# A fused two-part transformer kernel: modulation loads issued singly, four mixer products ahead of the norm, a fixed order in the router, and one more projection of layer 1 from the un-normed x

## The chip, the cores and the metric

One core of one Trainium2 chip runs the whole program. The metric is the device time of one execution in microseconds; the kernel before was timed three times. All products are made on TensorE (PE), elementwise work on VectorE (DVE) and ScalarE (ACT), a few copies on GpSimd (POOL). SyncE (SP) issues the weight loads, POOL's queue the modulation loads.

## The reference, cut to what matters

The input x is 256 tokens by 1024. It passes two hybrid layers, a final norm, one mixer block and one mixture of experts (MoE). All of it is float32.

```python
# one hybrid layer (twice)
mod = silu(c) @ ada_w + ada_b                       # six vectors: sh_m, sc_m, g_m, sh_f, sc_f, g_f
h = rms_norm(x, norm_mix_g) * (1 + sc_m) + sh_m
proj = h @ w_in                                     # NA, MLA and GQA inputs, three gates
o_na, o_mla, o_gqa = ...                            # three kinds of attention
merged = sigmoid(ga)*(o_na @ w_br_na) + sigmoid(gb)*(o_mla @ w_br_mla) + sigmoid(gc)*(o_gqa @ w_br_gqa)
x = x + g_m * (merged @ w_out)
h = rms_norm(x, norm_ffn_g) * (1 + sc_f) + sh_f
gate, up = split(h @ ffn_w_gate_up)
x = x + g_f * ((silu(gate) * up) @ ffn_w_down)
# after both layers
x = rms_norm(x, final_norm_g)
# mixer: RG-LRU, gated delta rule (GDN), stick-breaking attention, gated linear attention (GLA)
m = sum_n sigmoid(merge_n) * (y_n @ w_branch[n]);  x = layer_norm(alpha*x + m @ w_out)
# MoE: 16 experts in 4 groups; the best group, then the top 2 experts in it
scores = sigmoid(x @ w_router);  y = sum over chosen e of w_e * (silu(x@w_gate[e]) * (x@w_up[e])) @ w_down[e]
out = layer_norm(alpha*x + y)
```

In the mixer, the GDN input passes a causal convolution of four taps before its chunked recurrence, and so does the RG-LRU input.

## The kernel before, in words

**Products.** Activations lie transposed, 1024 features as eight slices of 128 partitions by 256 tokens. A float32 product is made of three matmuls: each operand is split into a high part rounded to the PE's format and a low part, the rest (`mm3`). A block of 128 output columns is 8 slices by 3 matmuls of 256 tokens, so 24; a load of 256 columns is 48. Products go to PSUM tiles of one bank; the tags are mm (two buffers), s (two), t (two), o and ad (one each).

**Weights.** `raw` has SP load up to 1 MB into one of three slots (`wr`); `pieces` makes the high part on ACT (a cast, into one of five `wh` slots) and the low part on DVE (a subtraction, into one of five `wl` slots). A raw slot is free for the next load when the subtraction has read it. `load` does both for 256 columns. Three lists change the order: `s.behind` holds a piece's cast behind a given instruction, `s.hold` holds the next subtractions behind given instructions, `s.defer` collects subtractions that are issued later.

**Order.** A list scheduler puts each engine's instructions into one order when the program is built; at run time an engine takes them in that order and waits for data and for slots. `s.after` adds an order without a wait. `post` and `step` put generators (attention, heads) between the blocks of a projection.

**Modulation.** The vectors of layer 0 that are needed first come from matmuls; the others from `ada`: a load of 0.5 MB on POOL's queue into one of ten `big` slots, and one DVE multiply and sum. `tick`, called by every `raw`, advances the generator; here two loads (`pace` 2) in each tick, in the order of the program on POOL, where the four copies of kg stand as well.

**Layer 1's start.** `norm_add` has already prepared z = x times gain, in high and low parts, with two extra columns for the shift. `zblock` multiplies a weight with z and afterwards scales the result by r = 1/rms; the shift's product comes out of column 256 and is added on ACT by the caller. So these products need no norm. `rstd` makes r from a matmul by Ln and Exp on ACT and a Newton step of three DVE operations (L252 to L254). In layer 1 the MLA latents are made that way; the GQA, NA and gate projections use the normed h from `norm_parts`.

**Layer 1's attention.** The GQA projection has three blocks, then NA's q and k (evacuated at L734) and v. `s.behind = evac` holds the casts of w_uq and w_ukv behind the evacuation of NA's k; the weights of the gates and of the next projection (labelled L_att in the profile) follow.

**Mixer.** `final_norm` writes z times r over x in eight slices, each with its splits; r lives in a `wl` slot. The two RG blocks multiply the un-normed z and scale by r (L1492). The misc block (beta, decay and low-rank columns) does so too, but in bank mm, after them; GDN's six blocks use the normed x.

**Router.** `out_norm` makes both token blocks' layer norm, the router's logits and the start of the MoE sum (matmuls with alpha times the identity). `route` chooses experts on DVE with some twenty small operations; `moe` builds placement matrices P and gathers tokens by matmul. Subtractions of the first experts' weights were deferred and are issued among them.

## Time and profile before

| | us |
|---|---|
| median of three runs | 1578.55 (1578.36 to 1579.76) |
| profiled execution | 1578.81 |
| its span, first to last instruction | 1577.1 |
| PE busy in the span | 1515.9 (96%) |
| DVE busy | 1199.1 (76%) |
| ACT busy | 902.7 (57%) |

The mean granted clock of PE was 0.986 of full speed. Busy times are of one execution; L12 is line 12 of the kernel. In a timeline, a row has the start, the time taken by all of the x instructions in the row, engine, line, operation, output and inputs, and in brackets how long the engine had been idle and what ended that. PEclk is the clock granted to PE, 1.00 being full speed.

### The profile page before, as it was taken

The page shows a single profiled execution, that of the slowest core. Times are in us where ns is not written, and L with a number is a line of the kernel's source. Part 1 is how long each engine was busy: PE and PEld are TensorE (multiplying, and loading weights), DVE is VectorE, ACT ScalarE, POOL GpSimd, SP SyncE. Part 2 cuts the span into 40 slices and gives each one's busy share as a digit, 9 for nine tenths or more (in the row PEclk, how much of TensorE's full clock was granted, in tenths as well). Part 3 has the DMA queues.
Part 4 walks back from the last instruction along what each step waited for, and adds up shares of the span by engine and source line. Part 5 has one row for each costly group of instructions (what it writes and reads, how often), then busy time and mean ns, then how long its engine had stood idle before and what let it go on. Part 6 is the DMA issues. An engine that isn't in the chain of part 4 may idle for free.

```text
span 1577.1 us, 27664 instructions
## 1 busy us (share of the span) xinstructions
PE 1515.9 (96%) x11216; PEld 1397.5 (89%) x11216; DVE 1199.1 (76%) x1760; ACT 902.7 (57%) x1316; POOL 100.7 (6%) x173
## 2 busy tenths in 40 slices
PE   6999999999997999999998999999999899999996
PEld 5889999999986989999997989989999688888884
DVE  5899789776785997975558875566666798888896
ACT  5565555444563554644446662675555477777774
POOL 0211000000001110000000022122000000000000
PEclk9999999999998999999999999999999999999998
DMA  9879676876446876565554640335656499999992
GB/s 348 283 238 305 198 240 200 308 267 215 134 141 231 288 241 212 183 208 188 187 174 143 188 126 9 117 103 157 186 175 227 160 324 330 330 330 331 332 346 79
DMA packets 206197, 346.27 MB, mean 220 GB/s; under 512 B 6944, under 2 KB 175024, under 8 KB 193776
## 3 DMA queue, kind: packets, MB, share of 16 engines
q1 hardware_dynamic: 191040, 294.42, 56.0%
q0 software_dynamic: 12656, 46.16, 8.3%
q10 hardware_dynamic: 2368, 3.86, 0.7%
q8 instruction: 90, 1.47, 0.4%
q14 instruction: 43, 0.35, 0.1%
HBM read 343.36 MB, written 1.05 MB: 218 GB/s over the span
## 4 chain that ended last, share of the span: by engine, by line
PE 68%; issue 23%; DVE 4%; DMA 3%; ACT 2%; POOL 0%; ACTq 0%; DVEq 0%; POOLq 0%; SPq 0%
PE L_gu.mm L195 5%; PE L_gu.mm L197 5%; PE L_gu.mm L196 5%; PE L_att.mm L195 3%; PE L_att.mm L197 3%; PE L_att.mm L196 3%; PE M_merge.mm L197 2%; PE M_merge.mm L195 2%; PE M_merge.mm L196 2%; PE L_gu.s L196 2%; PE L_gu.s L195 2%; PE L_gu.s L197 1%; PE L_gu.t L197 1%; PE L_gu.t L196 1%; PE L_gu.t L195 1%
## 5 line engine op out<-in xcount | busy, mean ns | idle before, releaser
L197 PE MATMUL L_gu.mm<-L_fnorm.hh,L_gu.wl 128*128 128x256 f32 x640 | 179.0, 280 | 0.0
L196 PE MATMUL L_gu.mm<-L_fnorm.hl,L_gu.wh 128*128 128x256 f32 x640 | 178.8, 280 | 0.0
L195 PE MATMUL L_gu.mm<-L_fnorm.hh,L_gu.wh 128*128 128x256 f32 x640 | 178.1, 279 | 0.0
L170 DVE TENSOR_TENSOR E_gu.wl<-E_gu.wr,E_gu.wh 128x1024 fp32r<-128x1024 f32 x124 | 150.1, 1224 | 21.2 <-ACT E_gu.wh L163 16.8
L170 DVE TENSOR_TENSOR L_gu.wl<-L_gu.wr,L_gu.wh 128x1024 fp32r<-128x1024 f32 x84 | 102.7, 1224 | 70.8 <-ACT L_gu.wh L163 70.3
L163 ACT CAST E_gu.wh<-E_gu.wr 128x1024 fp32r<-128x1024 f32 x124 | 129.7, 1054 | 40.0 <-PE E_gu.mm L197 11.7
L163 ACT CAST L_gu.wh<-L_gu.wr 128x1024 fp32r<-128x1024 f32 x84 | 88.2, 1050 | 112.4 <-PE L_gu.mm L196 70.5
L195 PEld LDWEIGHTS L_gu.mm<-L_fnorm.hh,L_gu.wh 128*128 128x128 f32 x640 | 120.2, 188 | 0.4 <-ACT L_fnorm.hh L310 0.4
L197 PEld LDWEIGHTS L_gu.mm<-L_fnorm.hh,L_gu.wl 128*128 128x128 f32 x640 | 120.5, 188 | 0.0
L196 PEld LDWEIGHTS L_gu.mm<-L_fnorm.hl,L_gu.wh 128*128 128x128 f32 x640 | 120.0, 188 | 0.0
L398 DVE SCALAR_TENSOR_TENSOR ada.big<-ada.big,L_mlaup.crow 128x1024 f32<-128x1024 f32 x80 | 95.9, 1218 | 0.0
L163 ACT CAST L_down.wh<-L_down.wr 128x1024 fp32r<-128x1024 f32 x48 | 50.5, 1052 | 75.3 <-PE L_gu.mm L196 39.8
L170 DVE TENSOR_TENSOR L_down.wl<-L_down.wr,L_down.wh 128x1024 fp32r<-128x1024 f32 x48 | 58.4, 1224 | 38.3 <-ACT L_down.wh L163 38.3
L163 ACT CAST L_att.wh<-L_att.wr 128x1024 fp32r<-128x1024 f32 x44 | 46.3, 1052 | 66.2 <-PE L_att.mm L196 35.7
L170 DVE TENSOR_TENSOR E_down.wl<-E_down.wr,E_down.wh 128x1024 fp32r<-128x1024 f32 x64 | 75.7, 1223 | 5.1 <-ACT E_down.wh L163 4.9
L163 ACT CAST E_down.wh<-E_down.wr 128x1024 fp32r<-128x1024 f32 x64 | 66.3, 1057 | 15.7 <-PE E_down.mm L197 6.5
L170 DVE TENSOR_TENSOR M_merge.wl<-M_merge.wr,M_merge.wh 128x1024 fp32r<-128x1024 f32 (+1 forms) x50 | 48.2, 969 | 30.5 <-ACT M_merge.wh L163 30.5
L405 POOL DMA_DIRECT2D ada.big<-in_ada_t x80 | 42.2, 529 | 390.2 <-DVE ada.big L398 200.9
L163 ACT CAST M_merge.wh<-M_merge.wr 128x1024 fp32r<-128x1024 f32 (+1 forms) x50 | 41.9, 843 | 44.0 <-PE M_merge.mm L196 38.3
L197 PE MATMUL M_merge.mm<-fnorm.hh,M_merge.wl 128*128 128x256 f32 x208 | 59.2, 284 | 0.0
L195 PE MATMUL M_merge.mm<-fnorm.hh,M_merge.wh 128*128 128x256 f32 x208 | 58.1, 279 | 0.0
L196 PE MATMUL M_merge.mm<-fnorm.hl,M_merge.wh 128*128 128x256 f32 x208 | 57.8, 278 | 0.0
(982 smaller groups left out, 5392.0 us busy)
## 6 DMA issues: line engine op xcount, KB each, us to landing
L_gu.wr<-in_w_gu SPq DMA_DIRECT2D x42, 1024.0 KB, 5.1
ada.big<-in_ada_t POOLq DMA_DIRECT2D x80, 512.0 KB, 5.8
E_gu.wr<-in_wu SPq DMA_DIRECT2D x32, 1024.0 KB, 5.1
E_down.wr<-in_wd SPq DMA_DIRECT2D x32, 1024.0 KB, 5.4
E_gu.wr<-in_wg SPq DMA_DIRECT2D x30, 1024.0 KB, 5.0
L_att.wr<-in_w_in SPq DMA_DIRECT2D x22, 1024.0 KB, 6.1
L_down.wr<-in_w_dn SPq DMA_DIRECT2D x22, 1024.0 KB, 4.9
M_merge.wr<-in_w SPq DMA_DIRECT2D x13, 1024.0 KB, 5.3
```

The lines of the kernel that those rows point to most:

```text
L163: c = s.nc.scalar.copy(hi, src).ins
L170: i = s.nc.vector.tensor_sub(lo, src, hi).ins
L195: mm(ps, ah, bh, start=first and fresh and k == 0, stop=False, skip_group_check=True)
L196: mm(ps, ah, bl, start=False, stop=False, skip_group_check=True)
L197: mm(ps, al, bh, start=False, stop=last and k == n - 1, skip_group_check=True)
L398: nc.vector.scalar_tensor_tensor(raw, raw, 0.5, s.crow, op0=ALU.mult, op1=ALU.mult, accum_out=sums[:, k:k + 1])
L405: s.tc.keep_in_program_order(nc.gpsimd.dma_start(raw, s.I["ada_t"][l, v, i % 8]))
```

## The change

Five edits, in the order of the program:

1. Modulation: `ada` gets `slow`; the first four ticks of layer's first generator issue one load each, then two again.
2. Layer 1: the first GQA block (256 columns) comes from `zblock`, its result is scaled and shifted in place and `gqa_heads` uses it without its own copy; the third and fourth weight subtractions after the norm are held behind the Newton step. The casts of w_uq and w_ukv are held behind the evacuation in layer 0 only.
3. Mixer: the weights of RG's second block, of misc and of one GDN block are loaded ahead; misc goes to bank s, this GDN block multiplies the un-normed z, goes to bank t and is scaled by r. r gets a tile of its own, three subtractions are held behind the norm's Newton step, and the splits of x are made for two slices at once. Two constants go (the -1e30 mask, now made from another mask, and the router's weights, now loaded into a mixer slot after `gla_decay`).
4. Router: the layer norm's application is made in halves of 512 at fixed places: for block 1, the last part is done in `route`, after the exponential and after the choice. The matmuls that start block 1's MoE sum follow the choice's matmuls.
5. MoE: the cast of block 1's high part is made in two halves; the deferred subtractions and the next two are held behind the placement matrices.

```diff
@@ -251,7 +251,7 @@
         nc.vector.scalar_tensor_tensor(t, ps, n * EPS, t, op0=ALU.add, op1=ALU.mult)
-        nc.vector.scalar_tensor_tensor(r, t, -3.0 * n, r, op0=ALU.add, op1=ALU.mult)
+        s.newton = nc.vector.scalar_tensor_tensor(r, t, -3.0 * n, r, op0=ALU.add, op1=ALU.mult).ins
         return r
...
@@ -382,7 +382,7 @@
-    def ada(s, vs, mods, pace, lag):
+    def ada(s, vs, mods, pace, lag, slow=0):
...
@@ -404,7 +404,7 @@
                 raws.append(raw)
-            if i % pace == pace - 1:
+            if i < slow or (i - slow) % pace == pace - 1:
                 yield False
...
@@ -505,7 +505,7 @@
-    def gqa_heads(s, i, p, qg, vc, gqk):
+    def gqa_heads(s, i, p, qg, vc, gqk, kept=False):
...
@@ -513,8 +513,10 @@
         nc.scalar.activation(sq[:, :wd], p[:, :wd], AF.Square)
-        pe = s.t([128, 512], "b2", NB)
-        nc.scalar.copy(pe[:, :wd], p[:, :wd])
+        pe = p
+        if not kept:
+            pe = s.t([128, 512], "b2", NB)
+            nc.scalar.copy(pe[:, :wd], p[:, :wd])
         if i == 2:
...
@@ -682,6 +684,7 @@
             r = s.norm_end()
+            s.hold = [None] * 2 + [s.newton] * 2
             h = s.norm_parts(x, r, s.zg, part(0))
...
@@ -716,13 +719,20 @@
         for i in range(3):
-            if l:
+            if l and i == 0:
+                w = s.load(w_in[:, 1184:1440], 8, 256)
+                p = s.t([128, 512], "b2", NB)
+                for j in range(2):
+                    v = p[:, j * 256:(j + 1) * 256]
+                    nc.scalar.activation(v, v, AF.Identity, bias=s.zblock(w[j], r, "mm", v))
+                    s.step()
+            elif l:
                 w = s.load(w_in[:, 1184 + i * 256:1440 + i * 256], 8, 256)
...
                 p = gqa(i)
-            s.post(s.gqa_heads(i, p, qg, vc, gqk))
+            s.post(s.gqa_heads(i, p, qg, vc, gqk, l and i == 0))
         LAB[0] = 'L_naqkv.'
...
@@ -754,9 +764,9 @@
             s.ada_row()
-        s.side = [s.ada([(l, v) for v in (4, 3, 2)], mods, 2, LAG[0])]
+        s.side = [s.ada([(l, v) for v in (4, 3, 2)], mods, 2, LAG[0], 4)]
         cut = lambda w, j: tuple(v[:, :, j * 128:(j + 1) * 128] for v in w)
-        s.behind = evac
+        s.behind = None if l else evac
         w = s.pieces(s.raw(I["w_uq"][l], 2, 512), (2, 512))
...
@@ -931,7 +941,6 @@
     o["ugt"] = (j > i)
-    o["mneg"] = np.where(i >= j, 0, -1e30)
     for b in (1, 2, 4, 8, 16, 32, 64):
...
@@ -1000,7 +1009,7 @@
     def proj(s, col0, x, ncol=256, w=None, bank="mm"):
-        w = s.load(s.I["w2"][:, col0:col0 + ncol] if w is None else w, 8, ncol)
+        w = w or s.load(s.I["w2"][:, col0:col0 + ncol], 8, ncol)
         p = s.acc(bank)
...
@@ -1019,15 +1028,26 @@
         nc = s.nc
-        r = s.t([128, 1024], "wl", WH, pool=s.w)[:, :256]
+        r = s.c.tile([128, 256], F32, name="zr")
+        s.ahead = s.ahead, s.load(s.I["w2"][:, 256:512], 8, 256)
         s.norm_end(out=r)
+        s.hold = [s.newton] * 3
+        s.ahead += s.load(s.I["w_misc"], 8, 128), s.load(s.I["w2"][:, OFF["gdn"] + 512:OFF["gdn"] + 768], 8, 256)
         s.zr = r
...
             nc.vector.scalar_tensor_tensor(xf[:, k], x[:, k], g[:, k:k + 1], r, op0=ALU.mult, op1=ALU.mult)
-            s.split(hi[:, k], lo[:, k], xf[:, k])
+            if k % 2:
+                s.split(*(v[:, k - 1:k + 1].rearrange("p a b -> p (a b)") for v in (hi, lo, xf)))
         return xf, hi, lo
+
+    def times_zr(s, p):
+
+        t = s.t([128, 512], "b2", NB2)
+        v = lambda t: t.rearrange("p (a b) -> p a b", a=2)
+        s.nc.vector.tensor_tensor(v(t), v(p), s.zr.unsqueeze(1).to_broadcast([128, 2, 256]), ALU.mult)
+        return t
...
@@ -1067,13 +1087,15 @@
         ident = s.cst["ident"]
-        p = s.proj(0, s.z, 128, I["w_misc"])
+        p = s.proj(0, s.z, 128, s.ahead[2], "s")
         misc = s.t([128, 256], "misc", 1)
...
         qkv = [s.b4() for _ in range(3)]
-        for i, bank in ((2, "mm"), (3, "ad"), (0, "mm"), (1, "o"), (4, "mm"), (5, "ad")):
-            p = s.proj(OFF["gdn"] + 256 * i, x, bank=bank)
+        for i, bank in ((2, "t"), (3, "ad"), (0, "mm"), (1, "o"), (4, "mm"), (5, "ad")):
+            p = s.proj(OFF["gdn"] + 256 * i, *((s.z, 256, s.ahead[3]) if i == 2 else (x,)), bank=bank)
+            if i == 2:
+                p = s.times_zr(p)
             dst = qkv[i // 2][:, (i % 2) * 512:(i % 2) * 512 + 512]
...
@@ -1138,7 +1160,7 @@
             dm = s.t([128, 512], "b2", NB2)
-            nc.vector.tensor_tensor(s.v4(dm), s.v4(ps), C["mneg"].unsqueeze(1).to_broadcast([128, 4, 128]), ALU.add)
+            nc.vector.scalar_tensor_tensor(s.v4(dm), C["ugt"].unsqueeze(1).to_broadcast([128, 4, 128]), -1e30, s.v4(ps), op0=ALU.mult, op1=ALU.add)
             for h in range(4):
...
@@ -1484,12 +1506,9 @@
         for i in range(2):
-            w = s.ahead if i == 0 else s.load(I["w2"][:, 256:512], 8, 256)
             pz = s.acc()
-            s.blocks(pz, w, s.z)
-            p = s.t([128, 512], "b2", NB2)
-            v = lambda t: t.rearrange("p (a b) -> p a b", a=2)
-            nc.vector.tensor_tensor(v(p), v(pz), s.zr.unsqueeze(1).to_broadcast([128, 2, 256]), ALU.mult)
+            s.blocks(pz, s.ahead[i], s.z)
+            p = s.times_zr(pz)
             for j in range(2):
...
@@ -1580,6 +1599,8 @@
         B = s.gla_decay(misc)
+        s.wr = s.t([128, 256], "misc", 1)[:, :128].rearrange("p (k n) -> p k n", k=8)
+        nc.gpsimd.dma_start(s.wr, s.I["w_rt"].rearrange("(k p) n -> p k n", p=128))
         gb = s.gate(OFF["gg"], x, g[:, 0])
...
@@ -1641,12 +1662,6 @@
         return s.t([128, 2, 2, 6], tag + "st", 1), s.t([128, 2, 2], tag + "mv", 1), s.t([128, 2], tag + "r", 1)
-
-    def norm_apply(s, out, z, mv, r, g, b, t, c):
-
-        nc = s.nc
-        nc.vector.scalar_tensor_tensor(out[:, t, c], z, mv[:, t, 0:1], g[:, c], op0=ALU.subtract, op1=ALU.mult)
-        nc.vector.scalar_tensor_tensor(out[:, t, c], out[:, t, c], r[:, t:t + 1], b[:, c], op0=ALU.mult, op1=ALU.add)
...
@@ -1712,11 +1727,24 @@
                     s.norm_stats(st, mv, r, ax[b], b)
+                    half = lambda q: (x2[:, b, q * 512:(q + 1) * 512], ax[b][:, q * 512:(q + 1) * 512], g[:, q * 512:(q + 1) * 512], bb[:, q * 512:(q + 1) * 512])
+
+                    def scaled(q):
+                        o, z, gq, _ = half(q)
+                        return nc.vector.scalar_tensor_tensor(o, z, mv[:, b, 0:1], gq, op0=ALU.subtract, op1=ALU.mult).ins
+
+                    def shifted(q):
+                        o, _, _, bq = half(q)
+                        return nc.vector.scalar_tensor_tensor(o, o, r[:, b:b + 1], bq, op0=ALU.mult, op1=ALU.add).ins
+                    scaled(0)
                     nc.vector.scalar_tensor_tensor(mr[:, b:b + 1], mv[:, b, 0:1], -1.0, r[:, b:b + 1], op0=ALU.mult, op1=ALU.mult)
                     nc.vector.scalar_tensor_tensor(u[:, b * 16:b * 16 + 16], s.csbw[:, :16], mr[:, b:b + 1], s.csbw[:, 16:], op0=ALU.mult, op1=ALU.add)
-                    for q in range(4):
-                        c = slice(q * 256, (q + 1) * 256)
-                        s.norm_apply(x2, ax[b][:, c], mv, r, g, bb, b, c)
+                    scaled(1)
+                    if b:
+                        s.x2 = shifted
+                    else:
+                        for q in range(2):
+                            shifted(q)
...
@@ -1727,19 +1755,18 @@
                 nc.vector.tensor_sub(xl[:, 0], x2[:, 0], xh[:, 0])
-        i = last[0]
         yp = [s.acc(t) for t in "sstt"]
-        for b in range(2):
+
+        def carried(b, i):
             for d in range(2):
...
                 i = j
-        return x2, xh, xl, yp, s.route(pr[:, :32], u, r)
+        carried(0, last[0])
+        return x2, xh, xl, yp, s.route(pr[:, :32], u, r) + (carried,)
     def route_weights(s):
-        s.wr = s.c.tile([128, 8, 16], F32, name="wrt")
-        s.late(s.nc.gpsimd.dma_start(s.wr, s.I["w_rt"].rearrange("(k p) n -> p k n", p=128)))
         s.rb = s.c.tile([128, 16], F32, name="rb")
...
@@ -1764,6 +1791,7 @@
         s.fn(sc, u, AF.Exp, scale=-1.0)
+        s.x2(0)
         nc.vector.tensor_scalar_add(sc, sc, 1.0)
...
@@ -1790,13 +1818,14 @@
         sel = s.c.tile([128, 32], BF16, name="sel")
-        nc.vector.scalar_tensor_tensor(v4(sel), v4(r), 2.0, gm.unsqueeze(2).to_broadcast([128, 8, 4]), op0=ALU.is_lt, op1=ALU.mult)
+        chosen = nc.vector.scalar_tensor_tensor(v4(sel), v4(r), 2.0, gm.unsqueeze(2).to_broadcast([128, 8, 4]), op0=ALU.is_lt, op1=ALU.mult).ins
...
         for b in range(2):
-            nc.tensor.matmul(pp[:, 32:48], s.onesb[:, 0], sel[:, 16 * b:16 * b + 16], start=False, stop=b == 1, skip_group_check=True)
+            at = nc.tensor.matmul(pp[:, 32:48], s.onesb[:, 0], sel[:, 16 * b:16 * b + 16], start=False, stop=b == 1, skip_group_check=True).ins
+        s.after(s.x2(1), chosen)
         pos, mx = (s.c.tile([128, n], F32, name=m) for n, m in ((16, "pos"), (1, "most")))
...
@@ -1806,7 +1835,7 @@
         nc.vector.tensor_reduce(mx, n8, axis=AX.X, op=ALU.max)
-        return sel, sc, pos, mx
+        return sel, sc, pos, mx, at
...
@@ -1821,10 +1850,10 @@
         ident = s.cst["ident"]
-        sel, sc, pos, mx = rt
+        sel, sc, pos, mx, at, carried = rt
         s.table(SILU)
         LAB[0] = 'E_gather.'
-        s.after(nc.scalar.copy(xh[:, 1], x2[:, 1]).ins, s.load_ins)
+        s.after(nc.scalar.copy(xh[:, 1, :512], x2[:, 1, :512]).ins, s.load_ins)
         f = lambda t: t.rearrange("p a b -> p (a b)")
...
@@ -1843,7 +1872,10 @@
             if g == 0:
+                nc.scalar.copy(xh[:, 1, 512:], x2[:, 1, 512:])
+                carried(1, at)
                 s.after(nc.vector.tensor_sub(xl[:, 1], x2[:, 1], xh[:, 1]).ins, i)
+                s.placed = i
                 todo = todo[::2] + todo[1::2]
...
@@ -1928,6 +1960,7 @@
         later, s.defer = s.defer, None
+        s.hold = [s.placed] * 2
         s.more = s.a
...
@@ -1942,7 +1975,7 @@
         for sub in later:
-            sub()
+            s.after(sub().ins, s.placed)
         tm = [token_map(0)]
...
```

## Rows read from the trace of the kernel before

**Rows 1.** The page's busy times: busy us (share of the span) x instructions

```profile
PE 1515.9 (96%) x11216; PEld 1397.5 (89%) x11216; DVE 1199.1 (76%) x1760; ACT 902.7 (57%) x1316; POOL 100.7 (6%) x173
```

**Rows 2.** PE's waits over the span: us in total, times, longest us

```profile
PE L_mlaup.mm L195 <- DVE L_mlaup.qf L768: 12.1, 3, 11.5
...
PE M_gdn.mm L195 <- DVE M_rg.b L1492: 3.8, 1, 3.8
PE E_route.o L1796 <- DVE sel L1793: 3.0, 1, 3.0
```

**Rows 3.** 25-us windows: width, busy us (instructions) of each engine, PEclk, DMA share, GB/s

```profile
425.00:450.00 25.00, 22.66 (x153) 21.40 (x152) 23.70 (x45) 15.60 (x34) 0.48 (x2) 0.86 0.50 153
500.00:525.00 25.00, 21.42 (x163) 20.75 (x164) 20.15 (x40) 15.82 (x33) 3.17 (x6) 0.84 0.73 230
850.00:875.00 25.00, 22.05 (x166) 19.40 (x167) 20.25 (x51) 17.08 (x30) 0.00 (x0) 0.88 0.49 148
875.00:900.00 25.00, 25.00 (x215) 25.00 (x214) 21.75 (x35) 17.69 (x27) 0.00 (x0) 1.00 0.66 204
1225.00:1250.00 25.00, 20.57 (x130) 15.78 (x130) 19.90 (x47) 10.17 (x15) 0.00 (x0) 0.93 0.35 123
1250.00:1275.00 25.00, 22.79 (x118) 19.90 (x118) 20.25 (x40) 14.83 (x18) 0.64 (x2) 0.93 0.79 287
```

**Rows 4.** Timeline of DVE around layer 1's norm

```profile
433.97 1.22 DVE L170 TENSOR_TENSOR L_gqaqkv.wl<-L_gqaqkv.wr,L_gqaqkv.wh 128x1024 fp32r<-128x1024 f32 x1
...
435.56 0.42 DVE L254 SCALAR_TENSOR_TENSOR L_norm.b<-L_norm.b,L_norm.b 128x256 f32<-128x256 f32 x1
```

**Rows 5.** Timeline of ACT, layer 1's attention

```profile
481.10 0.59 ACT L734 COPY L_naqkv.big<-L_gqaqkv.mm 128x512 f32<-128x512 f32 x1 [3.65 <-PE L_gqaqkv.mm L197]
...
499.98 1.04 ACT L163 CAST L_att.wh<-L_att.wr 128x1024 fp32r<-128x1024 f32 x1 [12.85 <-DMA L_att.wr<-in_w_in]
```

**Rows 6.** Timeline of SP, the same stretch

```profile
483.92 12.70 SPq L156 DMA_DIRECT2D L_att.wr<-in_w_in  x3
```

**Rows 7.** Timeline of POOL, the same stretch

```profile
480.92 1.76 POOL L788 COPY L_gqaatt.kg<-L_gqaqkv.qg 64x256 f32<-64x256 f32 x4 [30.31 <-DVE L_gqaqkv.qg L540]
482.63 3.13 POOL L405 DMA_DIRECT2D ada.big<-in_ada_t  x6
```

**Rows 8.** 2-us windows, columns as in rows 3

```profile
478.00:480.00 2.00, 2.00 (x16) 1.75 (x15) 1.17 (x4) 0.00 (x0) 0.00 (x0) 1.00 0.00 0
852.00:854.00 2.00, 1.05 (x5) 1.08 (x6) 2.00 (x5) 1.14 (x4) 0.00 (x0) 0.50 0.75 206
```

**Rows 9.** DMA queues from 486 to 489 us: packets, MB, share of 16 engines

```profile
q0 software_dynamic: 279, 1.02, 86.2%
q1 hardware_dynamic: 79, 0.08, 7.6%
```

**Rows 10.** DMA queues from 489 to 492 us, the same columns

```profile
q0 software_dynamic: 248, 0.92, 77.3%
q1 hardware_dynamic: 251, 0.26, 24.9%
```

**Rows 11.** Timeline of POOL, layer 0's attention

```profile
96.52 1.05 POOL L405 DMA_DIRECT2D ada.big<-in_ada_t  x2
```

**Rows 12.** Timeline of PE, start of the mixer

```profile
846.84 0.28 PE L197 MATMUL M_rg.mm<-L_down.hh,M_rg.wl 128*128 128x256 f32 x1
...
852.95 0.55 PE L195 MATMUL M_gdn.mm<-L_down.hh,M_gdn.wh 128*128 128x256 f32 x1 [3.83 <-DVE M_rg.b L1492]
```

**Rows 13.** Timeline of DVE, start of the mixer

```profile
842.28 1.22 DVE L170 TENSOR_TENSOR M_gdn.wl<-M_gdn.wr,M_gdn.wh 128x1024 fp32r<-128x1024 f32 x1
```

**Rows 14.** Timeline of DVE, the router

```profile
1241.85 1.17 DVE L168 TENSOR_TENSOR E_gather.wl<-E_gather.wr,E_gather.wh 128x1024 fp32r<-128x1024 f32 x1
...
1243.95 0.87 DVE L1648 SCALAR_TENSOR_TENSOR M_out.x<-M_out.b,M_out.lnmv,M_out.b 128x256 f32<-128x256 f32 x2
...
1246.55 1.22 DVE L170 TENSOR_TENSOR E_gu.wl<-E_gu.wr,E_gu.wh 128x1024 fp32r<-128x1024 f32 x1
```

## The prediction, made before the change was run

> **What bounds the kernel now.** I read the page's busy times first. TensorE (PE) is busy 1515.9 us of a span of 1577.1 [rows 1], so the engine that does the work is short of it for 61.2 us in all, and no edit here removes a matmul. What can be won is PE's idle time, and the time in which it ran at the lower of its two clocks. The waits of PE name three places that the diff touches: 11.5 us in one piece on the MLA query, 3.8 us at the mixer's start, 3.0 us on the router's choice [rows 2]. The windows of 25 us then give what each place lost [rows 3]: PE is busy 22.66 of 25 at a clock of 0.86 at the second layer's norm (425 to 450), the clock stands at 0.84 behind the big stall (500 to 525), PE is busy 22.05 at 0.88 at the mixer's start, 20.57 and 22.79 at 0.93 in the router. Between these stand windows like 875 to 900, 25.00 of 25 at clock 1.00: PE is the bound there, so what is won ahead of such a window is carried to the end. The full window has 215 matmuls, 0.117 us each; at the half clock (1.2 instead of 2.4 GHz) one takes twice that.
>
> The sum is made against the profiled execution: span 1577.1 us, run 1578.81 us (1.7 us lie around the span). That is 0.3 us above the median of 1578.55 and inside the runs' 1578.36 to 1579.76. A difference under about 0.2% (3 us) can't be told from no change.
>
> **A. Layer 1's norm: first GQA block from the un-normed x.** Lost here: 2.34 us idle, and at clock 0.86 some 3.5 us more, of which about 0.4 lie in the idle: 5.4 us at most [rows 3]. PE runs out of products from x and waits for parts of the normed h, which DVE makes one by one with 0.42 us operations, among subtractions of the weights' low halves of 1.22 us each. The change gives PE 48 matmuls (5.7 us) that need only the norm's input, and holds two such subtractions behind the norm's last Newton step; now one runs between the Newton steps, started at 433.97, ahead of the step at 435.56 [rows 4]. So r comes about 1.2 us earlier and h has 5.7 us more. Added: two DVE multiplications by r (0.42 us each by the same row), two activations and two tiny copies on ACT, two columns in each of 48 matmuls (under 0.1 us); removed: one ACT copy. DVE, full here, pays 0.84 us, and the half clock may stay for part of the stretch. I take 3.5 of the 5.4, bounds 0 and 5.4.
>
> **B. Layer 1's attention: cast freed from the evacuation, loads singly.** ACT waits 12.85 us for a weight (L_att.wr) and casts it at 499.98 [rows 5]; the softmax's exponentials stand behind that cast on ACT, DVE's reciprocal behind those, and PE's MLA query behind it. SP issues the load only at 483.92 [rows 6], because a raw slot is freed by the subtraction of w_uq, whose cast is held (s.behind) behind the evacuation at 481.10, ahead of which ACT stood idle 3.65 us [rows 5]. By then POOL, blocked by the copies of kg until 482.6, has sent six modulation loads of 0.5 MB in one burst [rows 7]. Two microseconds earlier (478 to 480) the DMA engines moved 0 GB/s [rows 8].
> The weight load then starves. From 486 to 489 us POOL's queue (q0) moved 1.02 MB and SP's (q1) 0.08 [rows 9]; from 489 to 492 0.92 against 0.26, with 248 packets against 251 [rows 10]. The Trainium skill (DMA: Bandwidth & Descriptors, section Queues, rings and completion order) says that each DMA engine takes turns between queue rows by packets, not by bytes; rows 10 agree with that, rows 9 don't (279 against 79 packets). By the rule alone, and with the 3.7 and 1.0 KB of a packet that rows 10 give, a burst of five loads (some 710 packets) against the 1024 of one weight would take 3.7 MB at some 390 GB/s, 9.5 us: a load still issued at 484 would land near 494 to 495, a gain of 5 to 6 us.
> After the change the cast of w_uq depends only on its own slot and data, so it can go into the 3.65 us that ACT stands idle, or before. Cast and subtraction then end by about 479 at the latest, SP issues at 475 to 480 into an idle DMA system, and the weight (1 MB, about 3 us at the 390 GB/s of these rows, plus a start of 2) is there before the burst bites. The price of moving the issue: nothing else is queued on SP ahead of it. The singly issued loads (one for each of the first four ticks) shorten the burst from six to about five here and spread the sixteen loads over two ticks more. The gain is the wait of 11.5 us [rows 2], less about 1 us of exponentials and reciprocal that stay in line, and plus the half clock that followed (0.84 over 25 us is 4.0 us, about 2 of them in running matmuls) [rows 3]: 14 at most. I take 11.5. If the early issue fails, it is 0 to 6.
> In layer 0 the same generator now sends only two loads, not four, ahead of its kg copies. Two followed those copies at 96.52 [rows 11]; now up to four do, beside SP's weights. That stage runs without a long wait today; I charge 0.3 us, bounds a gain of 1 and a loss of 13.8 (the stall of layer 1 over again).
>
> **C. Mixer start: four early products.** PE's last product from the un-normed x starts at 846.84, and the next stretch of work at 852.95, with two short matmuls in between; the long wait (3.83) is for a PSUM bank that DVE's evacuation frees [rows 12]. Lost: about 5.7 us idle, and at half clock until about 856 another 1.6, 7.3 together; the window's clock of 0.88 fits [rows 3]. The two RG blocks run from the un-normed x already; the change lets misc (24 matmuls, now in a bank of its own kind) and one GDN block (48) follow them: 72 by 0.117 is 8.4 us, which covers 846.9 to 855.3. Its r gets a tile of its own and so gives back one of five low-half slots, and three subtractions are held behind the Newton steps; today two run between them, one at 842.28 [rows 13], so r comes about 2 us sooner. Pairing the splits halves their count at one and a half times the length. Against it: DVE is busy 2.00 of 2 us here [rows 8], gets one more multiplication of 0.64, and has conv and evacuations in line behind it. What is late next is DVE's own queue. I take 4.5, bounds 2 and 7.3. The constants removed pay the tile; the router weights' load, now late in the mixer, is needed some 200 us later and is hidden by all that PE work.
>
> **D. Router.** Idle is 4.43 us in one window and 2.21 in the next, and clock 0.93 in both costs about 2 more in running matmuls: cap 8.8 [rows 3]. DVE does this chain one by one. In it stand deferred subtractions of 1.17 and 1.22 us that the router doesn't need (1241.85, 1246.55), and a third like them; and the second token block's scaling in eight operations of some 0.43 (two in the row at 1243.95) [rows 14]. The change holds the subtractions behind the placement matrices and puts four double-width scalings into DVE's waits. Removed from the chain: 3.6 us of subtractions and about 1.5 of scaling; they come back behind the gather, where PE has gather matmuls to run. The mask by multiply instead of add costs the same pass. I take 4.3, bounds 2 and 6.
>
> **Sum.** 3.5 + 11.5 + 4.5 + 4.3 - 0.3 = 23.5 us; 1578.8 - 23.5 = 1555.3.
>
> **Rivals.**
> First: the weight still starves. The scheduler may leave SP's load behind the burst, or the earlier weight only moves the wait to the second. For it: six loads are ready to go as soon as kg is copied [rows 7], and the change takes away one. Against: ACT idle and DMA idle just before [rows 5, 8]. B is then 0 to 6, the time 1578.8 - 12.0 - 3 = 1564, from 1561 to 1567. By the rule of the Trainium skill named above it would be 1561 to 1562.
> Second: DVE becomes the bound. A and C keep a third of their gain, since DVE is full in both (23.70 of 25 at the norm) [rows 3]; they give 2.7 in place of 8.0: 1560.6.
> Third, on the other side: the stall moves to layer 0. If its attention weight is sent behind a burst of four loads, as layer 1's stands behind six, 13.8 us are lost there; with layer 1's own stall kept (B at 0), 1578.8 - 12.0 + 13.8 = 1580.6. It decides when the new stall costs over 12 us and layer 1's stays. Against: four loads are 2.1 MB, 5.4 us at 390 GB/s, so a stall of that size needs both.
> Fourth: nothing moves, since the scheduler gives each engine nearly the order of before: 1577 to 1580. Against: the holds and the early products are fixed dependencies.
>
> **How the numbers follow.** The forecast as summed (1547 to 1560) has a chance of 0.57, the starved weight 0.20, DVE as the bound 0.13, the stall in layer 0 0.05, no change 0.04; 0.01 is left for other losses. The range goes from 1546 (every stage near its cap but the router: 5.4 + 14 + 7.3 + 6 = 32.7) to 1567 (a starved weight with B at nothing), which leaves out the third and fourth rivals. Faster by over 0.2%: 0.57 + 0.20 + 0.13 = 0.90; within 0.2%: 0.04; slower: 0.05 + 0.01 = 0.06. The predicted time is the sum, 1555.
>
> **What would show it.** In the profile after: no PE wait on the MLA query over 2 us, the first attention weight's issue ahead of 480 on SP (counted as before), and its cast without a wait of over 10 us; three or fewer microseconds of waits at the norm; PE full until the x products of the mixer, with no wait on the M_rg evacuation; the choice of the experts 2 us or more sooner behind w_out's last matmul, with no weight subtraction ahead of it; in layer 0 no new wait for L_att.wr above 3 us. The forecast is wrong if the attention weight's load keeps its place behind the burst, if the stall turns up again in layer 0, or if the four early products only move PE's wait behind them.

## The result, and the profile after

The changed kernel took 1556.62 us (median of four runs, 1555.18 to 1561.09) where the kernel before took 1579.15 beside it (1578.36 to 1581.09): a ratio of 0.986, 95% interval 0.9838 to 0.9883. It is faster by 22.5 us; 1555 was forecast, from 1546 to 1567. The profiled execution took 1555.92 us.

The page's first lines after the change, as in [rows 1]:

```profile
span 1554.2 us, 27654 instructions
...
PE 1509.2 (97%) x11216; PEld 1392.0 (90%) x11216; DVE 1197.2 (77%) x1751; ACT 904.6 (58%) x1316; POOL 104.1 (7%) x173
```

PE's idle time fell from 61.2 to 1554.2 - 1509.2 = 45.0 us, and its busy time by 6.7 us with the same 11216 matmuls: the mean granted clock rose from 0.986 to 0.994. Its waits in the changed stages, as in [rows 2]:

```profile
PE E_route.o L1824 <- DVE sel L1821: 2.8, 1, 2.8
PE L_gqaqkv.mm L197 <- DVE L_gqaqkv.wl L170: 1.9, 2, 1.4
...
PE M_gdn.ad L197 <- DVE M_gdn.wl L170: 0.9, 1, 0.9
PE L_gqaqkv.mm L195 <- DVE L_gqaqkv.b L319: 0.9, 1, 0.9
...
PE L_mlaup.mm L195 <- DVE L_mlaup.qf L778: 0.5, 2, 0.3
```

The 11.5 us on the MLA query are gone and the 3.8 us on M_rg's evacuation too; the wait for the router's choice has hardly changed (3.0 to 2.8). The same stretches in windows of 25 us, as in [rows 3] (the later ones lie some 13 and 20 us earlier now):

```profile
425.00:450.00 25.00, 22.01 (x169) 20.66 (x168) 23.36 (x48) 19.98 (x43) 1.72 (x2) 1.00 0.41 127
475.00:500.00 25.00, 24.49 (x185) 21.52 (x183) 18.86 (x36) 13.29 (x27) 5.95 (x13) 1.00 0.88 295
825.00:850.00 25.00, 24.06 (x196) 22.66 (x196) 22.75 (x57) 17.60 (x27) 0.00 (x0) 1.00 0.60 183
850.00:875.00 25.00, 24.92 (x213) 23.55 (x209) 24.17 (x40) 20.24 (x34) 0.00 (x0) 1.00 0.65 199
1200.00:1225.00 25.00, 21.59 (x163) 19.24 (x163) 17.17 (x38) 12.24 (x18) 0.00 (x0) 1.00 0.32 115
1225.00:1250.00 25.00, 23.68 (x111) 18.96 (x111) 21.10 (x41) 13.51 (x17) 0.72 (x2) 0.86 0.78 287
```

The clock of the norm, attention and mixer windows is 1.00 in this profile. Only the router still has a low one, 0.86.

Where the time came from is read by stages, from the start of one product on PE to the start of another in the timelines. Each kernel has the same marks: the last latent product of layer 1 (L_lat), the last NA product (L_naqkv), the first gate product (L_gates), layer 1's last gate/up product (L_gu), the first stick-breaking projection (M_sbin), w_out's last product (M_out), the experts' first product (E_gu) and the second one's bank (E_gu.mm). So the attention stage of before runs from 472.0 to 508.6, 36.6 us. The marks are rounded to 0.1 us, so a stage can be 0.1 off.

| kernel | norm: L_lat to L_naqkv | attention: to L_gates | mixer start: L_gu to M_sbin | router: M_out to E_gu | M_out to E_gu.mm |
|---|---|---|---|---|---|
| before | 33.9 | 36.6 | 68.2 | 19.8 | 38.1 |
| after | 31.1 | 25.3 | 60.9 | 17.5 | 36.1 |
| gain | 2.8 | 11.3 | 7.3 | 2.3 | 2.0 |

With 0.9 us lost ahead of the norm and 0.4 won behind E_gu.mm, these give the difference of the spans: 2.8 + 11.3 + 7.3 + 2.0 + 0.4 - 0.9 = 22.9. All else took the same time: from L_gates to L_gu 313.4 us in both, from M_sbin to M_out 348.1 in both.

The attention stage, on ACT, SP and POOL, as in [rows 5 to 7]:

```profile
470.31 1.05 ACT L163 CAST L_mlaup.wh<-L_mlaup.wr 128x1024 fp32r<-128x1024 f32 x1 [1.75 <-PE L_naqkv.mm L196]
...
485.69 1.05 ACT L163 CAST L_att.wh<-L_att.wr 128x1024 fp32r<-128x1024 f32 x1
```

```profile
472.64 13.92 SPq L156 DMA_DIRECT2D L_att.wr<-in_w_in  x3
```

```profile
478.70 1.77 POOL L798 COPY L_gqaatt.kg<-L_gqaqkv.qg 64x256 f32<-64x256 f32 x4 [26.29 <-DVE L_gqaqkv.qg L542]
480.42 2.62 POOL L405 DMA_DIRECT2D ada.big<-in_ada_t  x5
```

w_uq is cast at 470.31, ahead of the evacuation that it used to wait for. SP issues the first L_att.wr 2.3 us later (483.92 before). POOL's burst, now five loads, comes at 480.42, eight microseconds behind it; the weight's cast at 485.69 waits for nothing.

### The profile page after: what moved, and what is told of

Its sections match the earlier page's. It is cut to its first block, busy times and chain, and to the rows that moved or that the text cites. A ratio compares the mean times of both kernels' runs of the same rounds, so it can differ in the third digit from the quotient of the medians.

```text
span 1554.2 us, 27654 instructions
## 1 busy us (share of the span) xinstructions
PE 1509.2 (97%) x11216; PEld 1392.0 (90%) x11216; DVE 1197.2 (77%) x1751; ACT 904.6 (58%) x1316; POOL 104.1 (7%) x173
## 4 chain that ended last, share of the span: by engine, by line
PE 67%; issue 23%; DVE 5%; ACT 2%; DMA 1%; POOL 0%; DVEq 0%; ACTq 0%; POOLq 0%; SPq 0%
PE L_gu.mm L195 5%; PE L_gu.mm L197 5%; PE L_gu.mm L196 5%; PE L_att.mm L195 3%; PE L_att.mm L197 3%; PE L_att.mm L196 3%; PE M_merge.mm L195 2%; PE M_merge.mm L197 2%; PE M_merge.mm L196 2%; PE L_gu.s L196 2%; PE L_gu.s L195 2%; PE L_gu.s L197 2%; PE L_gu.t L197 1%; PE L_gu.t L196 1%; PE L_gu.t L195 1%
## 5 line engine op out<-in xcount | busy, mean ns | idle before, releaser
L163 ACT CAST E_gu.wh<-E_gu.wr 128x1024 fp32r<-128x1024 f32 x124 | 129.7, 1055 | 42.5 <-PE E_gu.mm L197 11.3
L170 DVE TENSOR_TENSOR L_att.wl<-L_att.wr,L_att.wh 128x1024 fp32r<-128x1024 f32 x44 | 53.4, 1219 | 8.4 <-ACT L_att.wh L163 8.2
```

The costliest lines, as they stand in the source:

```text
L163: c = s.nc.scalar.copy(hi, src).ins
L170: i = s.nc.vector.tensor_sub(lo, src, hi).ins
```

## The experiments

Each was timed beside the kernel before. Two executions of one kernel can differ by several microseconds (below), so parts of 2 us are read from the stages, not from the medians. A stage comes from one profile of each run. The stages of all:

| run | median us | norm | attention | mixer start | router | to E_gu.mm |
|---|---|---|---|---|---|---|
| e1_cast_free | 1568.26 | 34.9 | 24.9 | 68.8 | 20.1 | 38.4 |
| e2_singly | 1578.60 | 33.0 | 35.7 | 68.2 | 21.2 | 39.5 |
| e3_after_paired | 1557.51 | 32.1 | 24.4 | 61.0 | 17.4 | 35.9 |
| e4_after_gqa_h | 1558.38 | 33.3 | 25.6 | 60.9 | 18.0 | 36.6 |
| e5_after_gdn_x | 1559.67 | 31.1 | 25.3 | 64.0 | 17.3 | 35.8 |
| e6_after_subs_free | 1559.24 | 32.1 | 25.3 | 60.9 | 20.8 | 39.1 |
| e7_after_carry_late | 1554.87 | 31.1 | 25.2 | 60.9 | 17.0 | 35.3 |
| e8_after_load_first | 1557.58 | 34.9 | 23.9 | 60.9 | 18.6 | 37.2 |
| e9_after_again | 1558.40 | 32.8 | 25.3 | 60.9 | 17.5 | 36.1 |
| e10_carry_late_paired | 1556.84 | 32.7 | 24.5 | 61.1 | 18.4 | 36.7 |
| e11_after_fnorm_free | 1553.26 | 31.3 | 25.2 | 59.9 | 16.2 | 34.8 |
| e12_after_split_single | 1560.29 | 31.1 | 25.3 | 66.0 | 17.8 | 36.4 |

### The attention stall: issue time or size of the burst

**e1_cast_free**, the kernel before with one line:

```diff
-        s.behind = evac
+        s.behind = None if l else evac
```

> The kernel before, with one line changed: in layer 1 the casts of w_uq and w_ukv no longer wait for the evacuation of NA's k. Theory (the weight's load was issued too late, into POOL's burst): SP issues the first L_att.wr at 472 to 479 instead of 484, its cast on ACT waits under 2 us, PE's wait of 11.5 us on the MLA query is gone, and the gates start 11 to 13 us earlier: about 1567 us. Rival (the burst of six loads starves the weight whenever it is issued): most of the wait stays, 0 to 6 us won, 1573 to 1579 us.

SP, POOL, and PE's wait:

```profile
475.16 13.79 SPq L156 DMA_DIRECT2D L_att.wr<-in_w_in  x3
```

```profile
483.04 3.13 POOL L405 DMA_DIRECT2D ada.big<-in_ada_t  x6
```

```profile
PE L_mlaup.mm L195 <- DVE L_mlaup.qf L768: 0.2, 1, 0.2
```

The burst still has six loads, but the weight is issued 7.9 us ahead of it, and PE's wait falls from 11.5 to 0.2 us. The stage is 11.7 us shorter, the ratio to before 0.9927 (0.991 to 0.9945).

**e2_singly**, the kernel before with the other half:

```diff
-        s.side = [s.ada([(l, v) for v in (4, 3, 2)], mods, 2, LAG[0])]
+        s.side = [s.ada([(l, v) for v in (4, 3, 2)], mods, 2, LAG[0], 4)]
...
-            if i % pace == pace - 1:
+            if i < slow or (i - slow) % pace == pace - 1:
```

> The kernel before, with only the modulation loads of the first four ticks issued singly. Theory (issue time decides): L_att.wr is still issued at about 484 and still meets a burst, of five loads instead of six, so its cast comes 1 to 3 us sooner at most: 1576 to 1579 us. Rival (the size of the burst decides, weights and modulation loads taking turns packet by packet): 5 us or more won: 1573 us or less.

SP, POOL and ACT:

```profile
484.62 10.27 SPq L156 DMA_DIRECT2D L_att.wr<-in_w_in  x3
```

```profile
483.33 2.61 POOL L405 DMA_DIRECT2D ada.big<-in_ada_t  x5
```

```profile
498.39 1.04 ACT L163 CAST L_att.wh<-L_att.wr 128x1024 fp32r<-128x1024 f32 x1 [10.54 <-DMA L_att.wr<-in_w_in]
```

The weight is again issued behind the burst, waits 10.54 us instead of 12.85, and the stage wins 0.9 us. The ratio is 0.9999 (0.9986 to 1.0012).

**e3_after_paired**: the changed kernel with `slow` at 0.

> The changed kernel with the modulation loads again two in every tick. Theory: the first attention weight is loaded before the burst, so the size of the burst does not matter: within 1.5 us of the changed kernel, and PE's wait for the MLA query stays under 1 us in both layers. Rival (loads issued singly are needed as well): a PE wait of 3 us or more comes back at the MLA query or the attention of layer 1, 1560 us or more.

The attention stage took 24.4 us, 0.9 less than with single loads, and PE has no new wait in layer 0. e10 below, also with two loads in every tick, took 24.5, and the seven profiles with the same norm and attention and single loads took 25.2 to 25.3. So the earlier cast makes the whole gain of this part. Single loads won 0.9 us of the stage alone (e2), which the run's time does not show, and cost 0.8 us of it beside the earlier cast.

### The norm of layer 1

**e4_after_gqa_h**, the changed kernel without this part (the held subtractions included):

```diff
-            s.hold = [None] * 2 + [s.newton] * 2
...
-            if l and i == 0:
+            if False:
                 w = s.load(w_in[:, 1184:1440], 8, 256)
...
-            s.post(s.gqa_heads(i, p, qg, vc, gqk, l and i == 0))
+            s.post(s.gqa_heads(i, p, qg, vc, gqk))
```

> The changed kernel with layer 1's first GQA block made from the normed h again, and no subtraction held behind the Newton step. Theory from the trace after (layer 1's norm stage got 2.1 us shorter): the changed kernel plus 2 us, about 1559 us, with PE at the half clock again between 443 and 450. Rival (the prediction's 3.5 us for this part): 3.5 us slower, 1560 us. Third: the extra DVE work eats the gain, no difference, 1556 us.

The stage took 33.3 us against 31.1, 2.2 more, and the half clock was back there for a while. The stage itself scatters: 31.1 to 32.8 in the nine profiles with this part as changed (all but e1, e2, e4 and e8), 33.0 to 34.9 in the four without it (before, e1, e2, e4). So the part is worth about 2 us in the mean. Most of that is clock. From 440 to 460 us the granted clock was 1.00 in five of the nine (31.1 to 31.3 us) and 0.91 in the other four (e3, e6, e9 and e10: 32.1 to 32.8 us); without the part it was 0.91 in e2 and e4 (33.0 and 33.3 us) and 0.83 in the kernel before and e1 (33.9 and 34.9 us). At the same 0.91 the part is worth 0.2 to 1.2 us.

**e8_after_load_first** tried for the rest: it moves `norm_parts` behind the block's load, to have the subtractions first.

```diff
-            h = s.norm_parts(x, r, s.zg, part(0))
...
                 w = s.load(w_in[:, 1184:1440], 8, 256)
+                h = s.norm_parts(x, r, s.zg, part(0))
```

> The changed kernel, with layer 1's norm parts written behind the load of the first GQA block, so that its subtractions come ahead of them on DVE. Theory (PE's wait of 1.4 us in that block is the order on DVE): the wait is gone and the stage up to NA's last product is 1 to 2 us shorter. Rival (DVE is full from 436 to 454 us, so the wait moves to the normed h or to PSUM): less than 0.5 us, or slower.

PE's waits from 432 to 510 us in this kernel:

```profile
PE L_gqaqkv.o L246 <- DVE L_lat.b L253: 2.7, 1, 2.7
PE L_gqaqkv.mm L195 <- DVE L_gqaqkv.b L319: 1.1, 1, 1.1
```

The 1.4 us wait is gone, but one of 2.7 us stands behind it, for a Newton step on DVE, and the wait for the bank is 1.1 instead of 0.9. The stage is 3.8 us longer, of which some 1.7 are clock (0.89 from 460 to 475 us, 1.00 in the changed kernel), and the attention stage behind it 1.4 us shorter. The rival was right: DVE is full here (23.36 of 25 us in the changed kernel), and its order chose who waits.

### The mixer's start

**e5_after_gdn_x** takes the GDN block back to the normed x:

```diff
-            p = s.proj(OFF["gdn"] + 256 * i, *((s.z, 256, s.ahead[3]) if i == 2 else (x,)), bank=bank)
-            if i == 2:
-                p = s.times_zr(p)
+            p = s.proj(OFF["gdn"] + 256 * i, x, 256, s.ahead[3] if i == 2 else None, bank=bank)
```

> The changed kernel, but GDN's block i=2 is again multiplied from the normed x (its weight is still loaded ahead, its product still goes to bank t); RG's two blocks and misc stay from the un-normed x, the subtractions stay held and the splits paired. Theory (PE lacked products that need no norm): 48 matmuls by 0.117 us, 5.6 us, are gone from the gap, so PE idles 4 us or more before the first x product and runs at the half clock afterwards: 4 to 6 us more, about 1561 us. Rival (the earlier r and the paired splits made the gain, DVE being the bound): under 2 us more, 1557 to 1558 us.

PE's waits in this kernel from 815 to 890 us:

```profile
PE M_gdn.t L195 <- ACT fnorm.hh L237: 1.9, 2, 1.7
PE M_gdn.t L196 <- DVE fnorm.hl L238: 0.6, 2, 0.4
```

The stage is 3.1 us longer, where the eight profiles that have it as changed lie between 60.9 and 61.1: 48 matmuls earlier are worth 3.1 of the 7.3. The half clock that the theory expected behind the wait did not come. Neither theory had the number; the rest comes from elsewhere.

**e12_after_split_single** makes the splits of x one by one again.

```diff
-            if k % 2:
-                s.split(*(v[:, k - 1:k + 1].rearrange("p a b -> p (a b)") for v in (hi, lo, xf)))
+            s.split(hi[:, k], lo[:, k], xf[:, k])
```

> The changed kernel with the splits of the normed x made for one slice at a time again (eight casts and eight subtractions of 256 instead of four of 512). Theory: four more subtractions and casts, at some 0.36 for one of 256 against 0.6 for one of 512, put 0.5 us more on DVE's full queue: the mixer's start is 0.5 to 1.5 us longer. Rival (single splits hand the first slice over earlier, so PE starts sooner): no longer, or shorter by up to 0.5 us.

Its waits from 815 to 900 us, and a window of 8 us behind the first of them (columns as in [rows 3]):

```profile
PE M_gdn.ad L197 <- DVE M_gdn.wl L170: 1.8, 1, 1.8
PE M_gdn.mm L195 <- DVE M_rg.b L1048: 0.9, 1, 0.9
```

```profile
840.00:848.00 8.00, 7.06 (x34) 6.42 (x35) 8.00 (x29) 4.82 (x9) 0.00 (x0) 0.57 0.47 140
```

5.1 us more, five times what I had expected. Its two waits come to 2.7 us where the changed kernel has one of 0.9; that is 1.8. Behind them PE runs at the half clock (0.50 from 842 to 846, 0.57 from 840 to 848) where the changed kernel's is 1.00 and gets 58 matmuls done in those 8 us instead of 34; at 0.43 of 8 us that is the other 3.4. In e5 a wait of 1.7 us in the same stage brought no fall of the clock, so one profile does not show that the 3.4 belong to the splits. The order on DVE changed with the splits as well; the run does not separate the two.

**e11_after_fnorm_free** doesn't hold the three subtractions at the final norm.

```diff
-        s.hold = [s.newton] * 3
```

> The changed kernel, but the three weight subtractions at the final norm are not held behind its Newton step. Theory (of the 7.3 us won at the mixer's start, 3 came from the GDN block and 4 from DVE's earlier r and x): subtractions go between the Newton steps again, r comes 1 to 2.3 us later, and the stage from the last feed-forward product to the first stick-breaking projection is 1 to 2 us longer than 48.6. Rival (products from the un-normed x cover it): under 0.5 us longer.

The opposite came out, the stage is 1.0 us shorter. DVE in the changed kernel, and below it in this one:

```profile
828.43 0.42 DVE L252 TENSOR_TENSOR fnorm.b<-zr 128x256 f32<-128x256 f32 x1 [2.18 <-ACT zr L134]
...
829.35 0.42 DVE L254 SCALAR_TENSOR_TENSOR zr<-fnorm.b,zr 128x256 f32<-128x256 f32 x1
829.69 3.49 DVE L170 TENSOR_TENSOR fnorm.wl<-fnorm.wr,fnorm.wh 128x1024 fp32r<-128x1024 f32 x3
```

```profile
825.07 2.35 DVE L170 TENSOR_TENSOR fnorm.wl<-fnorm.wr,fnorm.wh 128x1024 fp32r<-128x1024 f32 x2
827.35 0.42 DVE L252 TENSOR_TENSOR fnorm.b<-zr 128x256 f32<-128x256 f32 x1
...
828.26 0.42 DVE L254 SCALAR_TENSOR_TENSOR zr<-fnorm.b,zr 128x256 f32<-128x256 f32 x1
```

In the changed kernel DVE stands idle 2.18 us ahead of the Newton steps, since the subtractions may not go first; in this one two of them (2.35 us) fill that time, and r is no later (from the start of PE's norm product, fnorm.o, to the last Newton step's start it is 2.95 and 2.96 us: 826.40 to 829.35, and 825.30 to 828.26). PE waits nowhere from 815 to 895 us but for 0.2.

### The router

**e6_after_subs_free** lets the weights' subtractions go where the scheduler puts them:

```diff
-        s.hold = [s.placed] * 2
...
-            s.after(sub().ins, s.placed)
+            sub()
```

> The changed kernel, but the deferred weight subtractions and the two after them are no longer held behind the placement matrices. Theory (subtractions in DVE's router chain cost what they last): two or three of 1.1 to 1.2 us go back in front of the choice, which comes 1 to 3.5 us later behind w_out's last matmul than the 7.7 us of the changed kernel: 1558 to 1560 us. Rival (PE's half clock and the matmuls behind the choice hide it): no difference over 1 us.

DVE in this kernel, with the three subtractions and the choice:

```profile
1218.92 1.21 DVE L168 TENSOR_TENSOR E_gather.wl<-E_gather.wr,E_gather.wh 128x1024 fp32r<-128x1024 f32 x1
...
1221.53 1.17 DVE L168 TENSOR_TENSOR E_gather.wl<-E_gather.wr,E_gather.wh 128x1024 fp32r<-128x1024 f32 x1
...
1224.97 1.22 DVE L170 TENSOR_TENSOR E_gu.wl<-E_gu.wr,E_gu.wh 128x1024 fp32r<-128x1024 f32 x1
...
1229.22 0.19 DVE L1821 SCALAR_TENSOR_TENSOR sel<-E_route.b 128x32 bf16<-128x32 f32 x1
```

The choice starts 11.3 us behind w_out's last product (1217.94), against 7.7 in the changed kernel, and the stage is 3.3 us longer: about what the three subtractions last (3.6). In this profile the router edit without the hold is slower than before (20.8 against 19.8).

**e7_after_carry_late** moves four matmuls. In the changed kernel, PE and DVE behind the choice:

```profile
1225.70 0.18 PE L1824 MATMUL E_route.o<-sel,M_out.b 128*128 128x32 bf16 x1 [2.83 <-DVE sel L1821]
...
1225.80 3.19 PE L1763 MATMUL M_ln.t<-M_out.x,M_out.b 128*128 128x512 f32 x4
1229.61 0.55 PE L1886 MATMUL E_gather.mm<-E_gather.P,M_out.hh 128*128 128x256 f32 x1 [0.62 <-issue]
```

```profile
1225.45 0.19 DVE L1821 SCALAR_TENSOR_TENSOR sel<-E_route.b 128x32 bf16<-128x32 f32 x1
...
1229.08 0.76 DVE L1870 TENSOR_TENSOR E_gather.P<-pos,cst 128x256 fp32r<-128x256 f32 x2 [2.25 <-PE M_ln.t L1763]
```

The four matmuls that start block 1's MoE sum (L1763) take 3.19 us, most of it at the half clock (e7 has them in 1.7 at the full one), and DVE stands idle 2.25 us for them ahead of the placement matrices. These name only pos and a constant as inputs, so what they wait for is memory: it frees when the matmuls have read their scaled identity, and in e7, which puts that elsewhere, the wait is gone.

```diff
-        aI = s.t([128, 512], "b2", NB2)[:, :128]
+        aI = s.zr[:, :128]
...
-                carried(1, at)
...
         for _ in steps:
             pass
+        carried(1, s.gathered)
```

> The changed kernel, with the matmuls that start block 1's MoE sum moved from before the gather to behind it, and their scaled identity put into the tile of r, so that the placement matrices no longer wait for its last reader. Theory (the gain of the router edit was given back by these matmuls: 3.2 us at the half clock, and the placement matrices waited 2.25 us for them): the gather begins 1.5 to 2.5 us sooner after the choice, the matmuls cost 0.9 us at full clock later, and the experts' first product begins 1 to 2 us sooner: 1555 us. Rival (the half clock stays until PE has worked a while, whatever it works on): the gather only runs slow earlier, 0 to 0.7 us won.

PE in this kernel:

```profile
1227.43 0.55 PE L1885 MATMUL E_gather.mm<-E_gather.P,M_out.hh 128*128 128x256 f32 x1 [1.62 <-DVE E_gather.P L1870]
...
1232.58 1.88 PE L1763 MATMUL M_ln.t<-M_out.x,zr 128*128 128x512 f32 x4
...
1234.66 0.48 PE L195 MATMUL E_gu.o<-E_gather.wh,E_gather.xgh 128*128 128x512 f32 x1
```

The gather begins 2.1 us sooner behind w_out's last product, yet the experts' first product only 0.5, and E_gu.mm 0.8. The four matmuls take 1.7 us at the full clock, not the 0.9 that I had worked out, and the gather begins at the half clock all the same. The rival was nearer. The gain is also smaller than the scatter of this stage: it took 16.2 to 18.6 us in the eight profiles that have the router as changed, and 18.4 in e10, which has e7's router.

**e10_carry_late_paired** adds e3's edit to e7's.

> The changed kernel with the late start of block 1's MoE sum and with modulation loads two in every tick, the two edits that looked free or useful. Theory (the stages add up): 0.6 to 1 us faster than the changed kernel beside it, all of it between w_out's last product and the experts' second one. Rival: nothing that can be measured, or a stall in layer 0 or 1 from the longer burst.

Beside it on the same chip stood **e9_after_again**, the changed kernel once more:

> The changed kernel once more, beside the next three on one chip: 1555 to 1558 us, and the stages as in its first profile (from layer 1's last latent product to the first gate product 56.4 us, from the last feed-forward product to the first stick-breaking projection 48.6, from w_out's last product to the experts' first 17.5).

e10 took 1556.84 us (1554.41 to 1559.98), e9 1558.40 (1554.57 to 1560.55): nothing that can be told apart, and e10's router was 0.9 us longer than e9's. e9's own norm stage was 1.7 us longer than in the first profile of the same kernel, and its layer 0 1.0 us (399.3 against 398.3, from the first GQA product to layer 1's last latent product). Windows of 10 us of the first profile, and below it of e9:

```profile
100.00:110.00 10.00, 10.00 (x87) 9.86 (x88) 10.00 (x17) 4.99 (x8) 1.82 (x4) 1.00 1.04 393
450.00:460.00 10.00, 9.88 (x75) 8.95 (x73) 9.97 (x12) 5.47 (x8) 2.42 (x2) 1.00 0.80 250
```

```profile
100.00:110.00 10.00, 9.66 (x67) 9.22 (x66) 9.28 (x17) 5.16 (x12) 2.10 (x4) 0.83 1.06 383
450.00:460.00 10.00, 8.42 (x51) 6.99 (x50) 9.64 (x12) 5.31 (x9) 4.13 (x3) 0.83 0.63 194
```

## Why the prediction was right, point by point

**Total.** 23.5 us were forecast against the profiled execution, 22.9 came. That is closer than its terms, and so by luck: two were too large by 0.7 and 2.0 to 2.3, one too small by 2.8, and these cancel.

**A, norm: 3.5 forecast, 2.8 in the two profiles, 2.2 by e4.** The early block runs without a gap in front, as forecast, and the clock is 1.00 in the first profile where 0.86 stood. But of the two things that the sum counted, idle time and clock, the idle time did not shrink: PE's waits from 432 to 473 us come to 4.4 us, where they had been 2.9. DVE remained full, and the waits moved to the block's second low half (1.4 us), a bank that DVE evacuates (0.9) and the heads' first steps (0.7 and 1.1). The gain is clock, and in four of nine profiles a part of it did not come (e4 above).

**B, attention: 11.5 forecast, 11.3 measured, 11.7 by e1 alone.** Cast, issue, burst and landing came in the order worked out; the issue, at 472.64, was still earlier than the 475 to 480 of the forecast. The first rival did not come: the load did not stay behind the burst (e1: six loads in it, no wait), nor did the wait move to the second weight, whose cast at 493.68 waited for no transfer.

The rule of the Trainium skill (DMA: Bandwidth & Descriptors, section Queues, rings and completion order), weighed in the prediction, is that each DMA engine takes turns between the queue rows by packets. The trace agrees with it where both queues move; packets, MB and share in the kernel before from 488 to 493 us:

```profile
q0 software_dynamic: 421, 1.54, 77.4%
q1 hardware_dynamic: 414, 0.42, 24.4%
```

The prediction read [rows 9] as against the rule. But SP's first packet moves only at 487.85 us, so for nearly two of those three microseconds its queue moved none. The landing that the prediction worked out for a burst of five, 5 to 6 us sooner, did not come all the same: e2 made that case and won 2.3 us on the weight's cast. What the working left out is the last part of the load. By the landings in the trace, 14 of the weight's 16 parts had landed from 495.5 to 496.0 us, one came at 498.4 and one at 499.96, and the cast of 499.98 waited for that one. In e2, which issued the weight 0.7 us later, 15 parts landed from 496.0 to 496.8 us and the last at 498.36, ahead of the cast of 498.39. So nearly all of the 2.3 us is the last part's; why it comes so late stays open.

**C, mixer: 4.5 forecast, 7.3 measured.** A size was off, and steps with it. The misc block did not follow the early products: the scheduler put it behind the first products from x (its last matmuls at 855.6), so 48 matmuls came early, not 72, worth 3.1 us (e5). r did come 2.0 us sooner after the norm product (2.95 us, where it had been 843.41 - 838.45 = 4.96), but not because of the hold, which costs 1.0 (e11). The largest difference, 5.1 us, came with the splits made singly (e12), a step that I had put at nothing: 1.8 of it are waits and 3.4 clock. Each piece was taken out with the others in place, so what they add up to need not be the whole. No run puts misc back into bank mm, for which PE had waited 3.83 us [rows 12]; what the change of banks is worth is not shown. The second rival, DVE as the bound, was right that DVE is full, and wrong that this keeps the gain small.

**D, router: 4.3 forecast, 2.0 to 2.3 measured.** The subtractions taken out gave 3.3 us (e6) of the 3.6 costed, and the choice came 4.6 us sooner behind w_out's last product: 1225.45 - 1217.78 = 7.7 us, where it had been 1250.58 - 1238.26 = 12.3. Half of that was given back. In the kernel before, block 1's four matmuls ran while PE waited for the choice anyway:

```profile
1246.69 1.10 PE L1735 MATMUL M_ln.t<-M_out.x,M_out.b 128*128 128x512 f32 x2 [0.23 <-DVE score L1767]
```

```profile
1250.58 0.19 DVE L1793 SCALAR_TENSOR_TENSOR sel<-E_route.b 128x32 bf16<-128x32 f32 x1
```

Now they stand behind the choice, mostly at the half clock, and the placement waits for them. The prediction costed the edit on DVE alone and forgot what it moved on PE. This is read from the rows: no run puts the matmuls back ahead of the choice, and e7, which moves them behind the gather, leaves them in PE's way. The stage also scatters with the clock, 16.2 to 18.6 us with the router as changed (eight profiles) against 19.8 to 21.2 in the three without it. (The terms of the forecast's cap add up to 8.6, not 8.8; the bounds did not use it.)

**E, layer 0: 0.3 forecast as a loss.** From the first GQA product to layer 1's last latent product it was 398.3 us in both, and the weight's cast waited 2.67 us as before. The third rival, a stall in layer 0, did not come. Nearly all of the 0.9 us lies ahead of that, where PE waits for the first loads (8.9 us in all, 8.6 before); the twelve further profiles have that point at 39.9 to 42.5 us, with the same work.

## What to carry to other kernels

A wait that names an engine or a transfer may have its cause in an order a dozen microseconds ahead: one line that lets a cast go earlier, and so a slot come free earlier, was worth half of the whole change, and the edit beside it that thinned the traffic nothing. Where one engine is full and another waits for its pieces, a new order on it can just choose who waits (e8); whether fewer instructions or their order made the gain at the mixer's start (e12) is not separated. A hold that keeps work out of an idle gap can cost what the work would have filled: 1.0 us here, and r came no sooner for it. Ask also what an edit moves on the engine that it does not mention: D's four matmuls. The version with the lowest median is the changed kernel without the hold at the final norm (e11): 1553.26 us (1552.18 to 1555.39), against 1558.40 (1554.57 to 1560.55) for the changed kernel on the same chip. Of that only the 1.0 us at the mixer's start lies where the code differs; in the profiles 1.3 more lies in the router, 1.5 in layer 1's norm and the rest ahead of it, where it is the same.

## What the runs showed of the hardware

The same instructions took different times by where the clock fell. The first profile of the changed kernel and e9 are one program, yet e9 has PE at 0.83 from 100 to 110 and from 450 to 460 us, with 1.00 in the first. In the router e11 and the changed kernel have the same order on PE, and its four matmuls of block 0, four of block 1 and the gather's start read:

```profile
1219.12 3.44 PE L1762 MATMUL M_ln.s<-M_out.x,M_out.b 128*128 128x512 f32 x4
...
1223.79 1.96 PE L1762 MATMUL M_ln.t<-M_out.x,M_out.b 128*128 128x512 f32 x4
1226.38 0.36 PE L1885 MATMUL E_gather.mm<-E_gather.P,M_out.hh 128*128 128x256 f32 x1 [0.62 <-issue]
```

Here the half clock came early and hit block 0's matmuls (3.44 us against 1.96), and block 1's took 1.96 instead of 3.19, the gather the full clock: 16.2 us for the stage instead of 17.5. Ahead of that fall PE had idled 0.60 and 0.68 us (the granted clock is 0.68 from 1218 to 1220 us, then 0.50); the changed kernel has the same two gaps, 0.61 and 0.68, and kept 1.00 behind them, until its wait of 2.83 us for the choice. So a gap of a given length does not decide it alone in these runs; what else does stays open. It also sets what a run can tell: the changed kernel alone spreads from 1554.6 to 1561.1 us.
